# Feed-forward products of a two-layer encoder on one Trainium2 core: the 512-column products of a step first, then the 256-column ones, with start addresses of their own for the weight parts

## The chip, the cores and the metric

The kernel runs on 1 core of one Trainium2 chip. The metric is the device time of one execution in microseconds. Before the change the median of 3 runs is 1233.04 us (1232.77 to 1233.06).

## The reference

The reference is a trunk of two layers over 256 tokens of width 1024, in float32. Each layer computes two half-step feed-forwards with a group of mixers and a cross-attention between them:

```python
for l in range(DEPTH):
    x = x + 0.5 * swiglu(rms_norm(x, ffn1_norm_g[l]), ffn1_w1[l], ffn1_w3[l], ffn1_w2[l])
    ...
    x = x + jnp.concatenate([ret, hgo, lru], axis=-1) @ w_out[l]
    x = x + cross_attention(rms_norm(x, xattn_norm_g[l]), rms_norm(mem, xattn_mem_g[l]), ...)
    x = x + 0.5 * swiglu(rms_norm(x, ffn2_norm_g[l]), ffn2_w1[l], ffn2_w3[l], ffn2_w2[l])
return rms_norm(x, final_norm_g)

def swiglu(h, w1, w3, w2):
    return (jax.nn.silu(h @ w1) * (h @ w3)) @ w2
```

The feed-forward width D_FF is 2816, so w1 and w3 are 1024 x 2816 and w2 is 2816 x 1024. The change concerns the four feed-forwards.

## The kernel before

**Split numbers.** Every large product is made of matmuls in fp32r. A float32 operand is split into a hi part (the value rounded to fp32r) and a lo part (the rest), and a product x w is computed as hi·hi + hi·lo + lo·hi. For the weights, `Weights._split` (from L107) does this for one step of up to 1024 columns per partition: ScalarE casts the raw weights to `w_hi` (L126) and VectorE subtracts to get `w_lo` (L127). Raw weights come by DMA from SyncE's queue (L99) into two buffers of 1 MB; `w_hi` and `w_lo` have three buffers each (PART_BUFS).

**Activations.** The tile `xn` holds, for each of 8 blocks of 128 features, the hi part of 256 tokens and then the lo part, 512 columns in a row; `g` holds the same for the 22 blocks of the inner width. So for one block of weights that TensorE has loaded, one matmul with 512 moving columns gives hi·hi and hi·lo at once, in the two halves of a PSUM bank, and one matmul of 256 columns with the lo part of the weights is added into the second half. `mm_w` (from L259) issues this pair:

```python
def mm_w(self, wh, wl, x, begin, stop):
    self.mm(self.ap, wh, x, begin, stop)
    self.mm(self.ap[:, 1, :], wl, x[:, 0, :], False, stop)
```

**Loops.** `ffn` walks over 11 column pairs of w1 and w3 (256 columns of the inner width at a time). For each of the two matrices, `gemm_w` takes the steps of the weights (a step holds 4 blocks of the contraction by 256 columns) and for each of two output banks and each block of the step it calls `mm_w`. The two matrices have 8 blocks of contraction, so two steps; w2 has 22, five steps of four and one of two. The very first column pair of the program uses `gemm_both`, with smaller steps (1, 1, 2, 2 and 2 blocks of both matrices). A bank is evacuated by a copy of its second half on ScalarE (L493) and an addition of the first half on VectorE (L494), or, after w2, by two additions into `xT` (L466).

**Who sets the order.** The Tile framework schedules the instructions by a simulation of its own, by priority and readiness, so the order on an engine is near that of the code, but a product may stand ahead of another where an operand is late. All matmuls go through `Bank.mm`, so they have the line L243 in the profile (L241 where `issue_after` is used; L245 in the changed file).

**Addresses.** The tiles `xn`, `g`, `w_hi` and `w_lo` are allocated with some spare elements and used from an offset in them (`XN_AT`, `G_AT` and `W_AT`, in elements of 4 bytes; `W_AT` by the weights' name). In the built program the buffers of `w_hi` and `w_lo` begin at 128 modulo 256 bytes, `xn` at 64 and `g` at 160; steps inside a tile are multiples of 512 bytes, so all products of a kind have the same start modulo 256. The offset for the weights of the feed-forwards is 16 (128 + 64 = 192), for `xn` 8 (64 + 32 = 96), for `g` 48 (160 + 192 = 352, which is 96).

**Other stages that the prediction reads.** The second matrix of the last feed-forward is computed the other way round (`gemm_x`, from L389): the activations are loaded, and hi and lo parts of 512 weight columns stream, all at 64 modulo 256. The keys of the cross-attention (`gemm_n` with `mem_n`) use products of 256 columns only, the moving operand at 64 and the weights at 32. The attention's scores (`k_mem` and `att`) are 256-column products with both operands at 160.

Of the kernel before, what the change touches and what calls it, by code (L numbers as in the profile page):

```python
# [9 lines left out]
F32R = mybir.dt.float32r  # L10
# [5 lines left out]
P = 128  # L16
D = 1024
S = 256
KD = D // P
# [5 lines left out]
CW = 256  # L25
# [5 lines left out]
PART_BUFS = 3  # L31
# [2 lines left out]
QE_BUFS = 1  # L34
T3_BUFS = 8
PAD = {"xn": 16, "g": 128, "mix": 0}
XN_AT = {"ffn1": 8, "mix": 8, "xattn": 8, "ffn2": 8}

W_AT = {("w13", False): 16, ("w1", False): 16, ("w3", False): 16, ("w2", False): 16, ("w2", True): 48,
        ("in", True): 56, ("kv", False): 40, ("kv", True): 48, ("out", False): 0, ("o", False): 0, "other": 48}  # L40
G_AT = (48, 40)
MIX_AT = 0
X_LOADS = ((0, 1), (1, 1), (2, 2), (4, 2), (6, 2))
T4_BUFS = 6
# [17 lines left out]
class Weights:  # L62
# [45 lines left out]
    def _split(self):  # L108
        nc, i = self.nc, self.n_split
        self.n_split += 1  # L110
        u, unit, at, nk = self.steps[i]
        while self.n_load < len(self.pieces) and self.pieces[self.n_load][0] <= u:
            self._load()
        at_ = W_AT.get((unit.key, unit.beside), W_AT["other"])
        hi = self.pool.tile([P, 4 * CW + 64], F32R, name="w_hi", tag="w_hi", bufs=PART_BUFS)[:, at_:at_ + 4 * CW]
        lo = self.pool.tile([P, 4 * CW + 64], F32R, name="w_lo", tag="w_lo", bufs=PART_BUFS)[:, at_:at_ + 4 * CW]
        if unit.key == "w13":
            hi, lo = (t[:, 0:2 * nk * CW].rearrange("p (h k c) -> p h k c", h=2, k=nk) for t in (hi, lo))
            t = self._both(u, at).rearrange("p (h k c) -> p h k c", h=2, k=nk)
        elif unit.beside:  # L120
            hi, lo = (t.rearrange("p (h k c) -> p h k c", h=2, k=2)[:, :, 0:nk, :] for t in (hi, lo))
            t = self.raw[u].rearrange("p h (k c) -> p h k c", k=4)[:, :, at:at + nk, :]
        else:
            hi, lo = (t.rearrange("p (k c) -> p k c", k=4)[:, 0:nk, :] for t in (hi, lo))
            t = self.raw[u].rearrange("p h (k c) -> p h k c", k=4)[:, at, 0:nk, :]
        self.last = nc.scalar.copy(hi, t)  # L126
        nc.vector.tensor_tensor(out=lo, in0=t, in1=hi.bitcast(F32), op=ALU.subtract)  # L127
        self.parts[i] = (hi, lo)
# [88 lines left out]
def trunk(ctx: ExitStack, tc: tile.TileContext, a: dict, out: bass.AP, stop=None, dbg=None):  # L217
# [9 lines left out]
    class Bank:  # L227
# [28 lines left out]
            self.mm(acc, lh, rl, False, False)  # L256
            self.mm(acc, ll, rh, False, stop)

        def mm_w(self, wh, wl, x, begin, stop):  # L259

            self.mm(self.ap, wh, x, begin, stop)
            self.mm(self.ap[:, 1, :], wl, x[:, 0, :], False, stop)

    class Act:

# [23 lines left out]
    def placed(pool, name, k, at, **kw):  # L289

        n = k * 2 * S
        return pool.tile([P, n + PAD[name]], F32R, name=name, bufs=1, **kw)[:, at:at + n].rearrange(
            "p (k u s) -> p k u s", k=k, u=2)
# [34 lines left out]
    vec_off, n = {}, 0  # L328
# [36 lines left out]
    def gemm_w(key, nk, x, banks):  # L365

        k0 = 0
        while k0 < nk:
            wh, wl, n = W.take(key)
            for m, bank in enumerate(banks):  # L370
                for k in range(n):
                    sl = slice(m * P, (m + 1) * P)
                    bank.mm_w(wh[:, k, sl], wl[:, k, sl], x[:, k0 + k], k0 + k == 0, k0 + k == nk - 1)
            k0 += n
            yield

    def gemm_both(x, pairs):

        k0 = 0
        while k0 < KD:  # L380
            wh, wl, n = W.take("w13")
            for u, banks in enumerate(pairs):
                for m, bank in enumerate(banks):
                    for k in range(n):
                        sl = slice(m * P, (m + 1) * P)
                        bank.mm_w(wh[:, u, k, sl], wl[:, u, k, sl], x[:, k0 + k], k0 + k == 0, k0 + k == KD - 1)
            k0 += n

    def gemm_x(key, nk, x, banks):  # L389
# [36 lines left out]
    class Norm:  # L426


        def __init__(self, l, name, mem=False):
            self.gains = col(l, name)  # L430
            if not mem:
                self.x = placed(keep, "xn", KD, XN_AT[name.split("_")[0]], tag="xn")
            self.ssq = small.tile([P, S], F32, name="ssq", tag="ssq", bufs=2)
# [38 lines left out]
    def ffn(l, f, nrm, nxt, last=False, setup=None):  # L472
        with tc.tile_pool(name="ffn", bufs=2) as fp:
            g = placed(fp, "g", KF, G_AT[last])
            if setup is not None:
# [35 lines left out]
            for c in range(0, KD, 2):  # L511
                banks = [mm_bank(2) for _ in range(2)]
                run(gemm_w("w2", KF, g, banks))
                for m in range(2):
                    add_tile(c + m, [banks[m][:, u, :] for u in range(2)], 0.5, nxt)
# [660 lines left out]
    for l in range(DEPTH):  # L1176
# [6 lines left out]
        with tc.tile_pool(name="kvp", bufs=1) as kvp, tc.tile_pool(name="mix", bufs=T4_BUFS) as mp:  # L1183
            nxt = Norm(l, "xattn_norm_g")
            k = mixer(l, nrm, nxt, mp, kvp)
# [104 lines left out]
```

## Time and profile before

| | |
|---|---|
| median of 3 runs | 1233.04 us |
| the profiled execution, its own time | 1232.75 us |
| its span (first to last instruction) | 1231.0 us |
| granted TensorE clock, mean | 0.998 |
| TensorE busy | 1220.6 us, 8378 matmuls |
| VectorE busy | 935.7 us |
| ScalarE busy | 738.3 us |
| DMA | 219.32 MB, mean 178 GB/s |

The profile is of one execution. Matmuls are pipelined, so the busy time of one overlaps that of the next; how long a product holds the engine is read from the distance of two starts in the timeline.

### The profile page before, as it was taken

To read this page: it belongs to the slowest core of one execution; us is meant where nothing else is said; L and a number is where in the kernel's file an instruction comes from. 1 tells how busy PE (TensorE), PEld (TensorE's weight loads), DVE (VectorE), ACT (ScalarE), POOL (GpSimd) and SP (SyncE) were. 2 spreads that over 40 slices of the span, in tenths; PEclk is the share of its full clock that TensorE was granted. 3 is DMA by queue.
4 is the path that set the end of the run, shared out by engine and by line. 5 is a ranking of instruction groups with operands and counts; after the bars stand their busy time and mean duration, and the time that the engine had idled before them with its cause. 6 is when DMAs were issued, how large, how long until landed. Compare 5 with 4: busy or idle time off the path is not lost.

```text
span 1231.0 us, 21670 instructions
## 1 busy us (share of the span) xinstructions
PE 1220.6 (99%) x8378; PEld 1100.8 (89%) x8378; DVE 935.7 (76%) x1649; ACT 738.3 (60%) x1309; POOL 30.5 (2%) x54
## 2 busy tenths in 40 slices
PE   9999999999999999999999999999999999999997
PEld 8888889988999988888888888899898999888886
DVE  6989866888777687786678886679787767778754
ACT  6766645556765665664466654465677646656643
POOL 1000000000100000000000000000000000000000
PEclk9999999999999999999999999999999999999999
DMA  7645555443344345455555455544434534555453
GB/s 253 251 182 190 173 190 200 146 163 138 137 173 171 125 184 200 177 205 188 189 216 204 177 200 188 188 171 155 155 138 146 196 137 155 192 185 200 177 188 120
DMA packets 62568, 219.32 MB, mean 178 GB/s; under 512 B 6912, under 2 KB 8192, under 8 KB 62208
## 3 DMA queue, kind: packets, MB, share of 16 engines
q1 hardware_dynamic: 60976, 213.35, 47.6%
q0 software_dynamic: 768, 3.86, 0.8%
q8 instruction: 66, 1.08, 0.3%
q10 hardware_dynamic: 720, 0.72, 0.2%
q14 instruction: 38, 0.31, 0.1%
HBM read 216.85 MB, written 1.05 MB: 177 GB/s over the span
## 4 chain that ended last, share of the span: by engine, by line
PE 95%; DVE 3%; ACT 1%; issue 1%; DMA 0%; POOLq 0%; POOL 0%; ACTq 0%; DVEq 0%
PE mm L243 87%; PE aux L243 2%; PE aux L833 1%; DVE w_lo L127 1%; DVE qe L814 0%; PE aux L831 0%; DMA xT<-in_x_t_dram 0%; PE mm L241 0%; ACT w_hi L126 0%; PE aux L241 0%; DVE xc L908 0%; PE aux L826 0%; PE aux L983 0%; PE aux L912 0%; PE aux L1104 0%
## 5 line engine op out<-in xcount | busy, mean ns | idle before, releaser
L127 DVE TENSOR_TENSOR w_lo<-w_raw,w_hi 128x1024 fp32r<-128x1024 f32 (+1 forms) x411 | 494.6, 1205 | 213.5 <-ACT w_hi L126 208.3
L126 ACT CAST w_hi<-w_raw 128x1024 fp32r<-128x1024 f32 (+1 forms) x411 | 425.1, 1035 | 360.5 <-PE mm L243 217.6
L243 PE MATMUL mm<-xn,w_hi 128*128 128x512 f32 (+1 forms) x2028 | 601.1, 359 | 1.6 <-ACT ssq L440 0.9
L243 PE MATMUL mm<-xn,w_lo 128*128 128x256 f32 x1728 | 476.9, 281 | 0.0
L243 PEld LDWEIGHTS mm<-xn,w_hi 128*128 128x128 f32 x2028 | 357.6, 188 | 57.2 <-ACT w_hi L126 1.1
L243 PEld LDWEIGHTS mm<-xn,w_lo 128*128 128x128 f32 x1728 | 324.7, 188 | 3.7
L243 PE MATMUL mm<-g,w_hi 128*128 128x512 f32 x528 | 180.8, 392 | 0.0
L243 PE MATMUL mm<-g,w_lo 128*128 128x256 f32 x528 | 141.9, 280 | 0.0
L243 PEld LDWEIGHTS mm<-g,w_hi 128*128 128x128 f32 x528 | 96.6, 188 | 19.0
L243 PEld LDWEIGHTS mm<-g,w_lo 128*128 128x128 f32 x528 | 99.4, 188 | 2.9
L243 PE MATMUL mm<-w_hi,xn 128*128 128x512 f32 (+1 forms) x318 | 89.1, 374 | 0.0
L493 ACT COPY f_p<-mm 128x256 f32<-128x256 f32 x176 | 63.8, 365 | 24.5 <-PE mm L243 23.6
L494 DVE TENSOR_TENSOR f_t<-mm,f_p 128x256 f32<-128x256 f32 x176 | 73.1, 418 | 2.5 <-ACT f_p L493 2.4
L243 PEld LDWEIGHTS mm<-w_hi,xn 128*128 128x128 f32 x318 | 57.2, 188 | 9.2
L498 DVE TENSOR_TENSOR f_t<-f_t,R 128x512 f32<-128x512 f32 x88 | 60.2, 688 | 1.6 <-ACT R L462 0.4
L243 PE MATMUL mm<-w_lo,xn 128*128 128x512 f32 (+1 forms) x160 | 56.6, 378 | 1.0 <-DVE w_lo L127 1.0
L243 PE MATMUL mm<-w_hi,g 128*128 128x512 f32 x176 | 51.9, 390 | 0.0
L243 PE MATMUL mm<-mem_n,w_hi 128*128 128x256 f32 x248 | 46.7, 284 | 0.0
L243 PE MATMUL mm<-o,w_hi 128*128 128x256 f32 x248 | 46.2, 281 | 0.0
L466 DVE SCALAR_TENSOR_TENSOR xT<-mm,xT 128x256 f32<-128x256 f32 x80 | 32.1, 420 | 17.3 <-PE mm L243 17.3
L243 PE MATMUL mm<-mix,w_hi 128*128 128x256 f32 x256 | 44.8, 279 | 0.0
L243 PE MATMUL mm<-w_hi,mem_n 128*128 128x512 f32 x128 | 39.5, 393 | 0.0
(253 smaller groups left out, 1476.6 us busy)
## 6 DMA issues: line engine op xcount, KB each, us to landing
w_raw<-in_weights_dram SPq DMA_DIRECT2D x395, 512.0 KB, 4.0
w_raw<-in_weights_dram SPq DMA_DIRECT2D x18, 256.0 KB, 3.6
m_t<-in_mem_t_dram POOLq DMA_DIRECT2D x2, 1024.0 KB, 6.4
xT<-in_x_t_dram SPq DMA_DIRECT2D x3, 256.0 KB, 6.4
cst<-in_c_cst_dram POOLq DMA_DIRECT2D x1, 696.0 KB, 4.4
out_dram<-yg SPq DMA_DIRECT2D x2, 320.0 KB, 2.5
gw<-in_gates_w_dram POOLq DMA_DIRECT2D x2, 256.0 KB, 6.8
fg<-in_final_norm_g_dram POOLq DMA_DIRECT2D x1, 512.0 KB, 5.8
```

The source lines that it names most:

```text
L126: self.last = nc.scalar.copy(hi, t)
L127: nc.vector.tensor_tensor(out=lo, in0=t, in1=hi.bitcast(F32), op=ALU.subtract)
L243: i = self.last = nc.tensor.matmul(acc, lhsT, rhs, start=begin, stop=stop, skip_group_check=True)
L466: nc.vector.scalar_tensor_tensor(out=xT[:, j, :], in0=h, scalar=scale, in1=xT[:, j, :], op0=ALU.mult, op1=ALU.add)
L493: nc.scalar.copy(p, banks[m][:, 1, :])
L494: nc.vector.tensor_tensor(out=t[m][:, u, :], in0=banks[m][:, 0, :], in1=p, op=ALU.add)
L498: nc.vector.tensor_tensor(out=t[m], in0=t[m], in1=nrm.R[:, None, :].to_broadcast([P, 2, S]), op=ALU.mult)
L833: nc.tensor.matmul(sb[bs, i, :], ke[:, 1 + i, cb], qe[:, 1 + i, cb], start=True, stop=True, skip_group_check=True)
```

## The change

`mm_w` now takes a list of the blocks of a step and issues all products with the hi part first, then all products with the lo part. `gemm_w` and `gemm_both` pass the list. `W_AT` has an offset each for the hi and the lo part; for the feed-forwards these are 48 and 40 instead of 16 and 16. The offset of `xn` is 0 instead of 8 in the feed-forwards, that of `g` is 40 instead of 48 in the first three.

```diff
-XN_AT = {"ffn1": 8, "mix": 8, "xattn": 8, "ffn2": 8}
-
-W_AT = {("w13", False): 16, ("w1", False): 16, ("w3", False): 16, ("w2", False): 16, ("w2", True): 48,
-        ("in", True): 56, ("kv", False): 40, ("kv", True): 48, ("out", False): 0, ("o", False): 0, "other": 48}
-G_AT = (48, 40)
+XN_AT = {"ffn1": 0, "mix": 8, "xattn": 8, "ffn2": 0}
+
+W_FF = (48, 40)
+W_AT = {("w13", False): W_FF, ("w1", False): W_FF, ("w3", False): W_FF, ("w2", False): W_FF, ("w2", True): (48, 48),
+        ("in", True): (56, 56), ("kv", False): (40, 40), ("kv", True): (48, 48), ("out", False): (0, 0),
+        ("o", False): (0, 0), "other": (48, 48)}
+G_AT = (40, 40)
...
-        hi = self.pool.tile([P, 4 * CW + 64], F32R, name="w_hi", tag="w_hi", bufs=PART_BUFS)[:, at_:at_ + 4 * CW]
-        lo = self.pool.tile([P, 4 * CW + 64], F32R, name="w_lo", tag="w_lo", bufs=PART_BUFS)[:, at_:at_ + 4 * CW]
+        hi = self.pool.tile([P, 4 * CW + 64], F32R, name="w_hi", tag="w_hi", bufs=PART_BUFS)[:, at_[0]:at_[0] + 4 * CW]
+        lo = self.pool.tile([P, 4 * CW + 64], F32R, name="w_lo", tag="w_lo", bufs=PART_BUFS)[:, at_[1]:at_[1] + 4 * CW]
...
-        def mm_w(self, wh, wl, x, begin, stop):
-
-            self.mm(self.ap, wh, x, begin, stop)
-            self.mm(self.ap[:, 1, :], wl, x[:, 0, :], False, stop)
+        def mm_w(self, steps):
+
+
+            for wh, _, x, begin, stop in steps:
+                self.mm(self.ap, wh, x, begin, stop)
+            for _, wl, x, _, stop in steps:
+                self.mm(self.ap[:, 1, :], wl, x[:, 0, :], False, stop)
...
-                for k in range(n):
-                    sl = slice(m * P, (m + 1) * P)
-                    bank.mm_w(wh[:, k, sl], wl[:, k, sl], x[:, k0 + k], k0 + k == 0, k0 + k == nk - 1)
+                sl = slice(m * P, (m + 1) * P)
+                bank.mm_w([(wh[:, k, sl], wl[:, k, sl], x[:, k0 + k], k0 + k == 0, k0 + k == nk - 1)
+                           for k in range(n)])
```

`gemm_both` is changed in the same way. In the built programs the start addresses of the changed products, modulo 256 bytes, are:

| product | moving, loaded before | moving, loaded now |
|---|---|---|
| xn with w_hi, 512 columns | 96, 192 | 64, 64 |
| xn with w_lo, 256 columns | 96, 192 | 64, 32 |
| g with w_hi, 512 columns | 96, 192 | 64, 64 |
| g with w_lo, 256 columns | 96, 192 | 64, 32 |

No other product gets another address.

TensorE, in the middle of a feed-forward (layer 0, the second one; `mm_5204` is a bank, `w_hi_5143` and `w_lo_5144` the parts of one step), before:

```order
L243 MATMUL mm_5204<-xn_4326,w_hi_5143 128x512
L243 MATMUL mm_5204<-xn_4326,w_lo_5144 128x256
L243 MATMUL mm_5204<-xn_4326,w_hi_5143 128x512
L243 MATMUL mm_5204<-xn_4326,w_lo_5144 128x256
L243 MATMUL mm_5204<-xn_4326,w_hi_5143 128x512
L243 MATMUL mm_5204<-xn_4326,w_lo_5144 128x256
L243 MATMUL mm_5204<-xn_4326,w_hi_5143 128x512
L243 MATMUL mm_5204<-xn_4326,w_lo_5144 128x256
```

and now:

```order
L245 MATMUL mm_5204<-xn_4326,w_hi_5143 128x512 x4
L245 MATMUL mm_5204<-xn_4326,w_lo_5144 128x256 x4
L245 MATMUL mm_5204<-xn_4326,w_hi_5163 128x512 x4
L245 MATMUL mm_5204<-xn_4326,w_lo_5164 128x256 x4
L245 MATMUL mm_5205<-xn_4326,w_hi_5143 128x512 x4
L245 MATMUL mm_5205<-xn_4326,w_lo_5144 128x256 x4
```

The alternation of the two sizes has become groups of four of each. In the built program there are 394 runs of four 512-column products and 439 runs of four 256-column products; most others are runs of two, at the ends of w2, or longer ones.

TensorE in the first unit of the program (`gemm_both`; four banks, `w_hi_144` holds two blocks of both matrices), before:

```order
L243 MATMUL mm_164<-xn_126,w_hi_144 128x512
L243 MATMUL mm_165<-xn_126,w_hi_144 128x512
L243 MATMUL mm_166<-xn_126,w_hi_144 128x512
L243 MATMUL mm_167<-xn_126,w_hi_144 128x512
L243 MATMUL mm_164<-xn_126,w_lo_145 128x256
L243 MATMUL mm_164<-xn_126,w_hi_144 128x512
L243 MATMUL mm_164<-xn_126,w_lo_145 128x256
L243 MATMUL mm_165<-xn_126,w_lo_145 128x256
```

and now:

```order
L245 MATMUL mm_164<-xn_126,w_hi_144 128x512 x2
L245 MATMUL mm_165<-xn_126,w_hi_144 128x512 x2
L245 MATMUL mm_166<-xn_126,w_hi_144 128x512 x2
L245 MATMUL mm_167<-xn_126,w_hi_144 128x512 x2
L245 MATMUL mm_164<-xn_126,w_lo_145 128x256 x2
L245 MATMUL mm_165<-xn_126,w_lo_145 128x256 x2
L245 MATMUL mm_166<-xn_126,w_lo_145 128x256 x2
L245 MATMUL mm_167<-xn_126,w_lo_145 128x256 x2
```

Four 512-column products stood in a row here before, too; the last product of every bank of a step now stands behind all products with the hi part.

TensorE at the start of the second feed-forward of layer 0, where the last block of `xn` is first used (the fourth product with `w_hi_5024` of bank `mm_5087`), before:

```order
L243 MATMUL mm_5139<-xn_4326,w_hi_5112 128x512
L243 MATMUL mm_5087<-xn_4326,w_hi_5024 128x512
L243 MATMUL mm_5087<-xn_4326,w_lo_5025 128x256
L243 MATMUL mm_5088<-xn_4326,w_hi_5024 128x512
L243 MATMUL mm_5088<-xn_4326,w_lo_5025 128x256
L243 MATMUL mm_5087<-xn_4326,w_hi_5024 128x512
L243 MATMUL mm_5087<-xn_4326,w_lo_5025 128x256
L243 MATMUL mm_5088<-xn_4326,w_hi_5024 128x512
```

and now:

```order
L245 MATMUL mm_5139<-xn_4326,w_hi_5112 128x512
L245 MATMUL mm_5087<-xn_4326,w_hi_5024 128x512
L245 MATMUL mm_5088<-xn_4326,w_hi_5024 128x512
L245 MATMUL mm_5138<-xn_4326,w_hi_5112 128x512
L245 MATMUL mm_5139<-xn_4326,w_hi_5112 128x512
L245 MATMUL mm_5087<-xn_4326,w_hi_5024 128x512
L245 MATMUL mm_5087<-xn_4326,w_lo_5025 128x256 x4
```

The scheduler takes the 512-column products of four banks in turn, block by block, and the 256-column products of a bank come behind the last block. The orders of SyncE and GpSimd are the same as before; on VectorE and ScalarE a few evacuations and casts have changed places with their neighbours.

## Rows read from the trace of the kernel before

**Rows 1.** The page: span, and busy time of engines (share) xinstructions.

```profile
span 1231.0 us, 21670 instructions
PE 1220.6 (99%) x8378; PEld 1100.8 (89%) x8378; DVE 935.7 (76%) x1649; ACT 738.3 (60%) x1309; POOL 30.5 (2%) x54
```

**Rows 2.** The page: the chain that ended last, by engine and by line.

```profile
PE 95%; DVE 3%; ACT 1%; issue 1%; DMA 0%; POOLq 0%; POOL 0%; ACTq 0%; DVEq 0%
PE mm L243 87%; PE aux L243 2%; PE aux L833 1%; DVE w_lo L127 1%; DVE qe L814 0%; PE aux L831 0%; DMA xT<-in_x_t_dram 0%; PE mm L241 0%; ACT w_hi L126 0%; PE aux L241 0%; DVE xc L908 0%; PE aux L826 0%; PE aux L983 0%; PE aux L912 0%; PE aux L1104 0%
```

**Rows 3.** Windows of two feed-forwards: busy us by engine, clock, DMA share.

```profile
core 0: us, PE busy (x) PEld busy (x) DVE busy (x) ACT busy (x) POOL busy (x), PEclk, DMA share, GB/s
...
455.00:610.00 155.00, 155.00 (x896) 136.44 (x895) 116.46 (x182) 87.16 (x148) 0.00 (x0) 1.00 0.52 189
640.00:795.00 155.00, 155.00 (x895) 136.46 (x895) 120.40 (x194) 90.68 (x155) 0.00 (x0) 1.00 0.52 190
```

**Rows 4.** Groups of TensorE by form: xcount, busy us, mean ns, idle before.

```profile
L243 PE MATMUL mm<-xn,w_hi 128*128 128x512 f32 x1408 | 486.9, 393 | 1.6 <-ACT ssq L440 0.9 <-DVE xn L361 0.7
L243 PE MATMUL mm<-xn,w_lo 128*128 128x256 f32 x1728 | 476.9, 281 | 0.0
L243 PE MATMUL mm<-g,w_hi 128*128 128x512 f32 x528 | 180.8, 392 | 0.0
```

**Rows 5.** Timeline of TensorE in a feed-forward: start us, us, what.

```profile
499.92 0.39 PE L243 MATMUL mm<-xn,w_hi 128*128 128x512 f32 x1
500.15 0.28 PE L243 MATMUL mm<-xn,w_lo 128*128 128x256 f32 x1
500.27 0.39 PE L243 MATMUL mm<-xn,w_hi 128*128 128x512 f32 x1
...
503.04 0.39 PE L243 MATMUL mm<-xn,w_hi 128*128 128x512 f32 x1
```

**Rows 6.** Timeline of TensorE, last feed-forward's second matrix, 24 products between these.

```profile
1189.99 0.62 PE L243 MATMUL mm<-w_hi,g 128*128 128x512 f32 x2
...
1195.43 0.62 PE L243 MATMUL mm<-w_hi,g 128*128 128x512 f32 x2
```

**Rows 7.** Timeline of TensorE, the keys, 26 products between these.

```profile
302.32 0.39 PE L243 MATMUL mm<-mem_n,w_hi 128*128 128x256 f32 x2
...
305.35 0.28 PE L243 MATMUL mm<-mem_n,w_lo 128*128 128x256 f32 x1
```

**Rows 8.** Timeline of TensorE in the first unit: four in a row.

```profile
10.47 1.09 PE L243 MATMUL mm<-xn,w_hi 128*128 128x512 f32 x4
11.40 0.28 PE L243 MATMUL mm<-xn,w_lo 128*128 128x256 f32 x1
```

**Rows 9.** Timeline of TensorE, the attention's scores: six products (5 and 1).

```profile
391.25 0.76 PE L243 MATMUL aux<-k_mem,att 128*128 128x256 f32 x5
...
391.97 0.76 PE L243 MATMUL aux<-k_mem,att 128*128 128x256 f32 x5
```

**Rows 10.** Timeline of VectorE while the keys' weights are split.

```profile
305.23 1.23 DVE L127 TENSOR_TENSOR w_lo<-w_raw,w_hi 128x1024 fp32r<-128x1024 f32 x1 [1.09 <-ACT w_hi L126]
```

**Rows 11.** Timeline at the start of layer 0's second feed-forward.

```profile
432.73 0.64 PE L243 MATMUL mm<-xn,w_hi 128*128 128x512 f32 x2
...
436.16 1.28 DVE L361 SCALAR_TENSOR_TENSOR xn<-xT,vec,xn 128x256 fp32r<-128x256 f32 x3
...
440.87 0.39 PE L243 MATMUL mm<-xn,w_hi 128*128 128x512 f32 x1
```

**Rows 12.** Timeline of TensorE at the end of the first unit.

```profile
18.74 0.28 PE L243 MATMUL mm<-xn,w_lo 128*128 128x256 f32 x1
18.94 0.50 PE L243 MATMUL mm<-xn,w_hi 128*128 128x512 f32 x1
19.28 0.28 PE L243 MATMUL mm<-xn,w_lo 128*128 128x256 f32 x1
```

More of the change, by code (lines that the diff above doesn't have):

```diff
@@ L383, in gemm_both @@
                 for m, bank in enumerate(banks):
-                    for k in range(n):
-                        sl = slice(m * P, (m + 1) * P)
-                        bank.mm_w(wh[:, u, k, sl], wl[:, u, k, sl], x[:, k0 + k], k0 + k == 0, k0 + k == KD - 1)
+                    sl = slice(m * P, (m + 1) * P)
+                    bank.mm_w([(wh[:, u, k, sl], wl[:, u, k, sl], x[:, k0 + k], k0 + k == 0, k0 + k == KD - 1)
+                               for k in range(n)])
             k0 += n
```

## Prediction

> **What bounds the kernel now.** I read the page's first part, then the chain, then the windows of the feed-forwards. TensorE is busy for 1220.6 of the 1231.0 us; VectorE has 76% of the span [rows 1]. The chain that ended last lies on TensorE for 95%, and 87% of it is one helper line, L243, which issues the products [rows 2]. In two feed-forward stretches TensorE has no idle time at all (155.00 of 155.00 us) at a granted clock of 1.00, its 2.4 GHz level, while VectorE is at 116 to 120 us, ScalarE at 87 to 91 and DMA at about half [rows 3]. So in these stages nothing is waited for: the time is the number of products times the slot that each takes, from its start to the next one's start. (The "mean ns of one" is no slot: consecutive matmuls overlap in it.)
>
> I call a product of 512 columns H and one of 256 columns L. The change touches 1408 + 528 = 1936 H [rows 4] and as many L (the L row of xn, x1728, also holds 320 of the mixer and attention). In today's alternating order nine pairs start between 499.92 and 503.04, so a pair takes 3.12 / 9 = 0.3467 us; the H slot is 0.23 and the L slot 0.12 [rows 5]. The 1936 pairs are 671 us, more than half of the kernel. One nanosecond per pair is 1.9 us.
>
> **The change, part by part.**
>
> *Order.* It removes and adds no instruction, byte or semaphore; inside a step the four H of a bank now stand together and the four L behind them. Today's trace has stages that already run products of one size in a row, and they show what such slots cost. The second matrix of the last feed-forward runs H alone: 24 of them from 1189.99 to 1195.43, 226.7 ns each [rows 6]. The keys of the cross-attention run L alone: 26 from 302.32 to 305.35, 116.5 ns each [rows 7]. Together 343.2 against 346.7.
>
> *Addresses.* Those two stages differ from the changed products in where their operands begin. In the first, moving and stationary operand both begin at 64 modulo 256 bytes [rows 6]; in the second at 64 and 32 [rows 7]. Today's feed-forward products begin at 96 and 192, and in the one place where they stand four in a row, in the first unit, four H take 11.40 - 10.47 = 0.93 us, 232.5 each [rows 8]: more than the 230 of the alternation. So the order by itself, at the old addresses, is not a gain. The change gives H the pair 64 and 64, that of rows 6, and L the pair 64 and 32, that of rows 7. I therefore price an H followed by an H at 226.7 and an L followed by an L at 116.5. What speaks against it: in rows 6 the weights stream and the activations are loaded, in the changed products it is the other way round.
>
> *The two turns of each group.* An H followed by an L, and an L followed by an H, have no row at the new addresses. Bounds for the H: 226.7 [rows 6] and 232.5 [rows 8]; I take 230, the H of the alternation, which is followed by an L too [rows 5]. For the L, which now streams while a stationary operand is loaded from the same start modulo 256: the attention's scores are 256-column products with equal starts and take 0.72 / 6 = 120 ns [rows 9]; the other bound is 116.5. I take 117, today's L before an H [rows 5].
>
> *The sum.* A group of four pairs takes 4 x 346.7 = 1386.7 ns now, and then 3 x 226.7 + 230 + 3 x 116.5 + 117 = 1376.6: 10.1 less. There are 344 such groups in the first two matrices (8 in each of 44 column pairs, without the 8 of the first unit) and 5 in each of the 24 output tiles of the second matrix, 464 in all: 4.7 us. Groups of two (24 in the second matrix, 12 in the first unit) save 693.3 - 690.2 = 3.1 each, 0.1 us. With the dear turns (230 and 120) a group saves 7.1, and the whole is 3.3; with the cheap ones (226.7 and 116.5) 13.9, and the whole 6.7. Sum: 4.8 us, from 3.3 to 6.7.
>
> *Edits that I cost at nothing.* The cast and the subtraction write the same number of elements, 1024, to another start; a subtraction into w_lo takes 1.23 us where the offset is already 40 [rows 10]. If that were wrong, VectorE has 35 us of idle time in 155 [rows 3] as cover. The lo part is needed 3 x 0.23 = 0.7 us later in each step than today, which only adds slack; today's waits for it are already none in these stretches [rows 3].
>
> *Where cover is lost.* At the start of a feed-forward the tiles of xn arrive one by one, and an L of an early tile can no longer fill a wait for a later one, since it stands behind the four H. At the second feed-forward of layer 0 the last tile is written by 436.16 + 1.28 = 437.44, and the first H that needs it starts at 440.87 [rows 11]. In the new order 28 H and 16 L stand ahead of that H, 28 x 0.2267 + 16 x 0.1165 = 8.2 us from 432.73, so 440.9 again: 3.5 us of slack are kept, and I cost it at 0. In the first unit a bank's last product moves to the end, so its evacuation starts later; there TensorE waits some 0.2 us today (an L slot of 0.20 and an H slot of 0.34 instead of 0.12 and 0.23 [rows 12]). The two small products of the norm now stand in that place and fill part of it. Bounds: -0.2 us, the wait goes, and +0.2, it doubles; I take 0.
>
> *Against the clock.* The profiled execution took 1232.75 us (span 1231.0), 0.29 less than the median of 1233.04. 1232.75 - 4.8 = 1227.95, and 1228.2 on the scale of the median. 1228.2 is my forecast.
>
> **A rule that speaks against it.** Slots at one and the same clock differ with the start addresses: 226.7 against 232.5 for four or more H in a row [rows 6, 8]. The Trainium skill, "TensorE: Matmul & The Clock Gate", sections "Back-to-back issue gap" and "What happens when you issue a matmul", gives the gap as columns / 2.4 + 2.5 ns and says that loading the next weights takes no read bandwidth from the running product. By it a pair is 325 ns in every order and at every address, the change is worth 0, and the time stays 1233.0. The trace does not agree: no pair is at 325, and slots of one size are not equal.
>
> **The rivals.**
>
> *No change.* The slot goes with which operand streams, not with the addresses: 226.7 is a property of streaming weights. Then an H in a run of the changed products stays near 230 and an L near 117, a pair near 347, and the time is between 1232.5 and 1233.5. For it: every stage with 226.7 streams weights. Against it: if only that mattered, the H of rows 8 would be at 230 as well, and not at 232.5. The rule of the Trainium skill above ends at the same time.
>
> *Slower.* Standing in a row is what costs: the runs of the first unit repeat at the new addresses, because that is how activations stream past freshly loaded weights. A group is then 4 x 232.5 + 4 x 117 = 1398, 11.3 more than now, times 464 is 5.2 us: 1238.3. It decides from the point at which an H inside a run is over 229.7 (4 x 229.7 + 4 x 117 = 1386.8). For it: rows 8 is the only place in this trace with the same operands in the same order. Against it: the start pair there is 96 and 192, and every stage with equal starts runs H at about 227.
>
> *The order is not what it says.* The scheduler could take the runs apart; the built order shows runs of four H in 394 places and of four L in 439, with the rest mostly longer, so I give it nothing.
>
> **How the numbers follow.** A measurement of this kernel tells some 0.2% (2.5 us) from no change, so faster means under 1230.6 and slower over 1235.5. The forecast has 0.66, no change 0.25 (0.05 of it for a case between the two, in which only a part of the address gain comes and the time ends between 1230.6 and 1232.5), slower 0.09. The forecast's own range is 1226.1 (the cheap turns, and 0.2 us of wait gone) to 1229.9 (the dear turns, and 0.2 us of new wait). Up to 1233.2 the range takes in the no-change case, and 0.3 us below the cheap end allow for the reading of the rows, whose starts are given to 0.01 us; it leaves out the slower rival and little else: 1225.8 to 1233.2. Faster 0.66, same 0.25, slower 0.09.
>
> **What would show it.** In the second feed-forward of layer 0 the profile should show H in rows of four taking 0.91 us from first to last start plus one, and a group of eight repeating every 1.377 us instead of 1.387. TensorE should stay busy for the whole of such a stretch, and idle time should not move to L126 or L127. If H starts lie 0.230 apart, the no-change rival holds; at 0.2325, the slower one. If the slots come out as forecast but the span does not shrink by 4 to 5 us, a wait at a stage's start has taken it, and the first products on xn would show it.

## The result and the profile after

The changed kernel takes 1242.54 us (median of 5 runs, 1242.37 to 1243.21) where the kernel before took 1232.77 beside it (5 runs, 1232.39 to 1233.06). The ratio is 1.0080, interval 1.0069 to 1.0092: slower by 9.8 us. The forecast was 1228.2 with a range to 1233.2, so it is wrong in sign, and the time lies beyond the slower rival's 1238.3 too.

The page of the changed kernel, span and busy time of the engines, which answers to [rows 1]:

```profile
span 1240.8 us, 21657 instructions
PE 1230.1 (99%) x8378; PEld 1100.6 (89%) x8378; DVE 937.1 (76%) x1649; ACT 741.7 (60%) x1309; POOL 32.3 (3%) x54
```

The span grew by 9.8 and TensorE's busy time by 9.5, with the same 8378 matmuls. TensorE's idle time went from 10.4 to 10.7 us. So nothing new is waited for: the products themselves take longer.

The same windows as [rows 3], busy time by engine, clock and DMA share:

```profile
core 0: us, PE busy (x) PEld busy (x) DVE busy (x) ACT busy (x) POOL busy (x), PEclk, DMA share, GB/s
...
455.00:610.00 155.00, 155.00 (x881) 134.37 (x880) 115.55 (x181) 88.08 (x149) 0.00 (x0) 1.00 0.51 185
640.00:795.00 155.00, 155.00 (x880) 134.25 (x879) 120.31 (x195) 91.56 (x157) 0.00 (x0) 1.00 0.52 188
```

TensorE is busy throughout, at the same granted clock of 1.00, but it gets through 881 and 880 products in 155 us where it did 896 and 895: 1.7% fewer. The reader should compare the counts in brackets here; the busy column alone says nothing has changed.

The waits of TensorE, the longest ones (us in total, times, longest):

```profile
PE mm L245 <- DVE xn L358: 1.3, 1, 1.3
PE aux L329 <- DVE mhalf L331: 1.0, 1, 1.0
PE mm L245 <- DVE w_lo L129: 1.0, 2, 0.5
PE mm L245 <- DVE xn L366: 0.7, 1, 0.7
```

The wait for a subtraction was there before, by the same view:

```profile
PE mm L243 <- DVE w_lo L127: 1.0, 2, 0.5
```

No wait is over 1.3 us, and no idle time has moved to the casts or the subtractions (L128 and L129 now).

The timeline of TensorE in the second feed-forward of layer 0 (start, us from first start to last end, products in the row), where [rows 5] showed the alternation:

```profile
502.17 1.10 PE L245 MATMUL mm<-xn,w_hi 128*128 128x512 f32 x4
503.11 0.64 PE L245 MATMUL mm<-xn,w_lo 128*128 128x256 f32 x4
503.58 1.10 PE L245 MATMUL mm<-xn,w_hi 128*128 128x512 f32 x4
504.53 0.63 PE L245 MATMUL mm<-xn,w_lo 128*128 128x256 f32 x4
505.00 0.40 PE L245 MATMUL mm<-xn,w_hi 128*128 128x512 f32 x1
```

The order is what the change says: four H, four L. From 502.17 to 505.00 two groups pass, 1.415 us each; the forecast was 1.377 and the kernel before has 1.387. A row of four H takes 0.94 to 0.95 us, and not 0.91. With the trace's starts, averaged over some 300 rows of four H on xn, the four slots are 240.4, 237.2, 233.0 and 230.9 ns, and of the L 118.3, 119.0, 115.9 and 117.3. That makes 941.5 + 470.5 = 1412 ns a group, 25.3 more than before. The built order has 394 rows of four H: 394 x 25.3 = 10.0 us, the size of the whole loss. Adding up the slots of all products of both traces says the same without a mean: the 1408 H on xn take 7.5 us longer, the 528 H on g 2.2 us, and the L together no longer than before. The loss lies in the H.

### The profile page after: what moved, and what is told of

Read it like the earlier page. It is cut to its first block, busy times and chain, and to the rows that moved or that the text cites. A ratio compares the mean times of both kernels' runs of the same rounds, so it can differ in the third digit from the quotient of the medians.

```text
span 1240.8 us, 21657 instructions
## 1 busy us (share of the span) xinstructions
PE 1230.1 (99%) x8378; PEld 1100.6 (89%) x8378; DVE 937.1 (76%) x1649; ACT 741.7 (60%) x1309; POOL 32.3 (3%) x54
## 4 chain that ended last, share of the span: by engine, by line
PE 95%; DVE 2%; ACT 1%; issue 1%; DMA 0%; POOLq 0%; POOL 0%; SPq 0%; DVEq 0%; ACTq 0%
PE mm L245 88%; PE aux L245 2%; PE aux L838 1%; DVE w_lo L129 0%; DMA w_raw<-in_weights_dram 0%; PE aux L836 0%; ACT w_hi L128 0%; PE mm L243 0%; PE aux L243 0%; PE aux L831 0%; PE aux L988 0%; PE aux L917 0%; PE aux L1109 0%; PE aux L974 0%; DVE qe L819 0%
## 5 line engine op out<-in xcount | busy, mean ns | idle before, releaser
L129 DVE TENSOR_TENSOR w_lo<-w_raw,w_hi 128x1024 fp32r<-128x1024 f32 (+1 forms) x411 | 494.2, 1204 | 213.4 <-ACT w_hi L128 209.2
L128 ACT CAST w_hi<-w_raw 128x1024 fp32r<-128x1024 f32 (+1 forms) x411 | 424.9, 1034 | 344.0 <-PE mm L245 232.1
L245 PE MATMUL mm<-xn,w_hi 128*128 128x512 f32 (+1 forms) x2028 | 502.5, 362 | 1.9 <-DVE xn L358 1.3
L245 PEld LDWEIGHTS mm<-xn,w_hi 128*128 128x128 f32 x2028 | 336.9, 188 | 38.3 <-ACT w_hi L128 1.4
L245 PE MATMUL mm<-xn,w_lo 128*128 128x256 f32 x1728 | 313.7, 281 | 0.0
L245 PEld LDWEIGHTS mm<-xn,w_lo 128*128 128x128 f32 x1728 | 275.5, 188 | 30.2
L245 PE MATMUL mm<-g,w_hi 128*128 128x512 f32 x528 | 145.5, 396 | 0.0
L245 PEld LDWEIGHTS mm<-g,w_hi 128*128 128x128 f32 x528 | 89.7, 188 | 12.2
L245 PEld LDWEIGHTS mm<-g,w_lo 128*128 128x128 f32 x528 | 81.2, 188 | 12.1
L245 PE MATMUL mm<-g,w_lo 128*128 128x256 f32 x528 | 84.0, 280 | 0.0
```

Source lines behind the costliest of these rows:

```text
L245: i = self.last = nc.tensor.matmul(acc, lhsT, rhs, start=begin, stop=stop, skip_group_check=True)
```

## The experiments

The kernel before measured 1232.5 to 1232.8 us beside every run below. Slots are from the trace's starts, averaged over all rows of a kind on xn. "Settled" means the slot that a long row keeps from its sixth product on, the last product aside. Every edit is shown against the changed kernel; `...` marks lines left out.

### The two halves of the change alone

The order alone, at the old addresses:

```diff
-XN_AT = {"ffn1": 0, "mix": 8, "xattn": 8, "ffn2": 0}
+XN_AT = {"ffn1": 8, "mix": 8, "xattn": 8, "ffn2": 8}
...
-W_FF = (48, 40)
+W_FF = (16, 16)
...
-G_AT = (40, 40)
+G_AT = (48, 40)
```

> The new order (four H, then four L) at the addresses of before (96 and 192). Theory 'turns': an H costs 226.7 ns only once a run has settled, and every run of H pays behind a run of L, whatever the addresses; then this is slow as well, about 1238 to 1243 us, with H slots over 230 in every group. Theory 'addresses': the new start pairs are the loss; then this stays at 1233 us or below, and the four H of a group take no more than 920 ns.

Measured: 1242.70 us (1242.37 to 1243.24), ratio 1.0083 (1.0066 to 1.0100). H 231.2, 234.6, 233.4, 235.2; L 118.4, 118.4, 120.3, 118.3: 1410 a group.

The addresses alone, in the old order:

```diff
-            for wh, _, x, begin, stop in steps:
+            for wh, wl, x, begin, stop in steps:
                 self.mm(self.ap, wh, x, begin, stop)
-            for _, wl, x, _, stop in steps:
                 self.mm(self.ap[:, 1, :], wl, x[:, 0, :], False, stop)
```

> The old order (H, L, H, L) at the new addresses (64 and 64 for H, 64 and 32 for L). Theory 'turns': the alternation keeps its own rhythm, a pair stays within 1 ns of 346.7 and the time within 1231 to 1235 us. Theory 'addresses': the pair rises by some 5 ns as in the changed kernel, and the time is 1240 us or more.

Measured: 1242.53 us (1242.40 to 1242.58), ratio 1.0080 (1.0065 to 1.0095). H 232.9, L 120.1: 353.0 a pair. The timeline of the addresses alone, nine pairs between the rows:

```profile
500.14 0.40 PE L245 MATMUL mm<-xn,w_hi 128*128 128x512 f32 x1
...
503.33 0.39 PE L245 MATMUL mm<-xn,w_hi 128*128 128x512 f32 x1
```

3.19 / 9 = 354 ns, against 346.7 in [rows 5]. So each half costs some 10 us alone, and both together cost 10 and not 20. The halves do not add: neither "the turns of a row cost" nor "the addresses cost" explains the result without the other. Here the L lose as well: added up over the trace, the slots of all H grew by 6.0 us and those of the L by 4.0, which is the whole loss.

### Longer rows

Rows of eight: the H of both banks, then the L of both, at the new addresses.

```diff
+        def mm_hi(self, steps):
+            for wh, _, x, begin, stop in steps:
+                self.mm(self.ap, wh, x, begin, stop)
+
+        def mm_lo(self, steps):
+            for _, wl, x, _, stop in steps:
+                self.mm(self.ap[:, 1, :], wl, x[:, 0, :], False, stop)
...
             for m, bank in enumerate(banks):
-                sl = slice(m * P, (m + 1) * P)
...
+                bank.mm_hi(steps[m])
+            for m, bank in enumerate(banks):
+                bank.mm_lo(steps[m])
```

> At the new addresses all eight H of a step (both banks) come before all eight L. Theory 'turns': half as many turns; eight H take about 1832 ns and eight L about 931, as in the nine places of the changed kernel where this already occurs, 10 ns less than eight pairs in alternation, so about 1230 us, faster than before. Theory 'addresses': all H slots stay high (235 on the mean) and the time stays near 1242 us.

Measured: 1235.79 us (1235.13 to 1238.09), ratio 1.0026 (1.0017 to 1.0036). The loss falls from 9.8 to 3.1. The slots by place in the row, H: 232.8, 235.7, 228.3, 232.6, 230.5, 226.9, 226.7, 235.0. The sixth and the seventh are at the forecast's 226.7; the first five and the last are not.

The expected 1230 was missed by 6 us. It took eight H at 1832 ns from the nine places of the changed kernel where they stand in a row; here they take 1848.5. Those nine places stand among rows of other lengths (from the changed kernel's trace, at the end of an output tile of the second matrix):

```profile
577.99 0.63 PE L245 MATMUL mm<-g,w_lo 128*128 128x256 f32 x4
578.46 1.99 PE L245 MATMUL mm<-g,w_hi 128*128 128x512 f32 x8
580.29 1.10 PE L245 MATMUL mm<-g,w_lo 128*128 128x256 f32 x8
581.22 1.09 PE L245 MATMUL mm<-g,w_hi 128*128 128x512 f32 x4
582.14 0.64 PE L245 MATMUL mm<-g,w_lo 128*128 128x256 f32 x4
582.62 1.10 PE L245 MATMUL mm<-g,w_hi 128*128 128x512 f32 x4
583.56 0.63 PE L245 MATMUL mm<-g,w_lo 128*128 128x256 f32 x4
```

Eight H behind four L take 1.83 us here; four H take 0.92 us behind eight L and 0.94 behind four. Against 226.7 for each H, the nine rows of eight are 18 ns dearer and the nine rows of four behind them 19. In the kernel with rows of eight, rows of eight H that stand behind only four L are 55 ns dearer (15 rows), and those behind eight L 35. So what a row of H costs over the settled slot depends on the rows ahead of it.

Does streaming activations reach 226.7 at all? In this kernel every L is replaced by a second H with the same operands (the lo part of the weights is left out, and the hi part counted twice); the first feed-forwards have the new addresses, the second ones the old.

```diff
-            for _, wl, x, _, stop in steps:
-                self.mm(self.ap[:, 1, :], wl, x[:, 0, :], False, stop)
+            for wh, _, x, _, stop in steps:
+                self.mm(self.ap, wh, x, False, stop)
...
```

> The feed-forwards (but for the last second matrix) compute something else here: each product with the lo part of the weights is replaced by a second H with the same operands, so TensorE runs H alone; the first feed-forward of a layer is at the new addresses, the second one at those of before. The time is longer by the replaced columns and says nothing. Theory 'turns': an H at the new addresses takes 226.7 ns over hundreds of products, with activations streaming; at the old ones a run of H stays at about 232.5. Theory 'addresses': an H stays at 231 or more at the new ones too, since it is the streaming operand that decides.

Measured: 1451.79 us in one run, for 1936 products of 512 columns where there were 256. The timeline of TensorE, first a first feed-forward (40 H from xn, up to the first of g), then a stretch of a second one:

```profile
159.66 9.23 PE L247 MATMUL mm<-xn,w_hi 128*128 128x512 f32 x40
168.73 31.44 PE L247 MATMUL mm<-g,w_hi 128*128 128x512 f32 x138
```

```profile
574.63 65.76 PE L247 MATMUL mm<-xn,w_hi 128*128 128x512 f32 x280
```

At the new addresses 9.07 / 40 = 226.8 ns each, at the old (65.76 - 0.39) / 279 = 234.3. So in a long row 226.7 comes with the starts and not with the operand that streams, as the forecast had it; and long rows of H at 96 and 192 are dearer than the 230 of the alternation, which is why the order alone lost: its four H sum to 934.4, 233.6 each. That is not over the settled 234.3, so at the old starts the H of a row of four carry no price for the turn.

### The old order at other starts

A first theory after these runs was that a slot goes with the operand that is loaded beside it, which is the next product's. Three kernels in the old order, with the loop of "the addresses alone", and one in the new order, with other starts of hi and lo; of the edits only the starts are shown:

```diff
-W_FF = (48, 40)
+W_FF = (40, 48)
```

> The old order (H and L alternately), with the two starts of the weights exchanged: the hi part begins at 32 and the lo part at 64 modulo 256, activations at 64. Theory A, the load beside: a slot goes with the start of the streaming operand against the start of the stationary operand that is loaded beside it, which is the next product's. Beside an H the lo part (64) is loaded, equal starts: H 226.7; beside an L the hi part (32): L 116.5 to 117. A pair is 343.2 to 343.7, 3.0 to 3.5 less than the kernel before, over 1936 pairs 5.8 to 6.8 us: 1226 to 1227. Theory B, the product's own load: a slot goes with the start of its own stationary operand: H at 64 with 32 gives 233, L at 64 with 64 gives 120, a pair 353 as with the unexchanged starts: 1242.5. Theory C, the rhythm: changing sizes in turn costs, whatever the starts, so a pair stays at 346.7 or more: 1233 or later.

Measured: 1229.63 us (9 runs, 1229.52 to 1229.97), ratio 0.9974 (0.9965 to 0.9984): 3.1 us faster than the kernel before, the best time of the study. H 227.3, L 118.0: 345.2 a pair (hi at 32, lo at 64). Its timeline, nine pairs:

```profile
499.86 0.39 PE L245 MATMUL mm<-xn,w_hi 128*128 128x512 f32 x1
500.08 0.28 PE L245 MATMUL mm<-xn,w_lo 128*128 128x256 f32 x1
500.20 0.39 PE L245 MATMUL mm<-xn,w_hi 128*128 128x512 f32 x1
...
502.95 0.39 PE L245 MATMUL mm<-xn,w_hi 128*128 128x512 f32 x1
```

3.09 / 9 = 343 ns here, 345.2 as the mean over all. Windows of the first feed-forward and of the one with these rows show part of the difference (busy time by engine, clock, DMA share):

```profile
30.00:185.00 155.00, 155.00 (x897) 136.59 (x896) 129.41 (x262) 97.19 (x173) 0.72 (x1) 1.00 0.54 196
455.00:610.00 155.00, 155.00 (x901) 137.26 (x900) 116.69 (x183) 87.45 (x148) 0.00 (x0) 1.00 0.53 190
```

In the first 100 us the same products with the same starts run H at 227 to 234 (means over 20 us), 231 in all, and from then on at 226 to 228: 897 products in the first window, 901 in the second. The sign is theory A's, but the L is dearer than it says, and the next three runs refute it. Theory C, which had 346.7 or more, falls here.

```diff
-W_FF = (48, 40)
+W_FF = (48, 48)
```

> The old order, hi and lo both beginning at 64 modulo 256, activations at 64. Theory A, the load beside: every product streams from 64 beside a load from 64: H 226.7, L 120, a pair 346.7, the same as the kernel before: 1233. Theory B, the product's own load: the same starts, so the same numbers. Theory C, the rhythm: an H after an L stays at 230 or more, a pair 350 or more: over 1239.

Measured: 1241.69 us (1240.88 to 1242.51), ratio 1.0072 (1.0053 to 1.0090). H 235.1, L 116.8. Every product has equal starts, its own and its neighbour's, and H is nowhere near 226.7. Theories A and B fall.

```diff
-W_FF = (48, 40)
+W_FF = (40, 40)
```

> The old order, hi and lo both beginning at 32 modulo 256, activations at 64. Theory A, the load beside, and theory B, the own load, agree here: H 233, L 116.5 to 117, a pair 349.5 to 350: 1238 to 1239. Theory C, the rhythm: no number of its own, 346.7 or more. With this run and the one with both at 64, the price of each of the four combinations stands alone; if the exchanged run is the sum of the cheap two, A holds.

Measured: 1233.66 us (1233.42 to 1233.90), ratio 1.0007 (0.9997 to 1.0017). H 228.8, L 118.2: 347.0 where A and B had 350.

The new order with `W_FF = (40, 48)`, hi at 32 and lo at 64:

> The order of the changed kernel (four H, then four L), with the two starts exchanged: hi at 32, lo at 64. Theory A, the load beside: three H of a group run beside a load from 32 and one beside a load from 64, three L beside 64 and one beside 32: 3 x 233 + 226.7 + 3 x 120 + 117 = 1403 per group, 16 more than the kernel before, 7.5 us: 1240. Theory B, the own load: 4 x 233 + 4 x 120 = 1412: 1244. Theory C, the rhythm: the first H after a run of L are slow whatever the starts, so 1410 as in the three arrangements seen so far: 1242 to 1243.

Measured: 1236.25 us (1235.93 to 1237.18), ratio 1.0029 (1.0018 to 1.0040). H 228.5, 234.9, 231.1, 235.5; L 116.2, 112.8, 116.9, 118.2: 1394 a group. No theory had that; A, at 1240, was the nearest and still 4 us off.

### All starts at once

In these two kernels the starts change from unit to unit of the first two matrices, through all 64 combinations; the first in the old order, the second in the new.

```diff
         at_ = W_AT.get((unit.key, unit.beside), W_AT["other"])
+        if unit.key in ("w1", "w3"):
+            n_ff = sum(k in ("w1", "w3") for k in self.keys[:u])
+            at_ = (n_ff % 8 * 8, (n_ff + n_ff // 8) % 8 * 8)
```

> The old order, activations at 64; in the first two matrices the starts of hi and lo change from unit to unit (16 pairs each) through all 64 combinations of 0, 32, ... 224 modulo 256; the second matrix as in the changed kernel. The slots by combination are read, not the time. Seen so far per pair (hi, lo): 64, 32: 353.0; 64, 64: 351.8; 32, 64: 345.2; 32, 32: 347.0. Theory D, the start of the part that H loads: the pair goes with hi, and lo moves it by less than 2 ns: eight columns of nearly equal numbers, from 345 to 353. Theory E, the distance between the two stationary starts: the pair goes with hi minus lo, so combinations of equal distance agree; the two equal starts seen so far, 351.8 and 347.0, speak against it. Theory F, history: the slot depends on the starts of all neighbours and on when each begins, so the table has no simple law and neighbouring combinations differ by up to 10 ns.

> The same scan in the order of the changed kernel, four H and then four L. Seen so far per group of four pairs (hi, lo): 64, 32: 1412; 32, 64: 1396; both at 192 with activations at 96: 1410. If a row of four could be priced from long rows by its own starts, as the prediction did, then hi 64 would give 4 x 226.7 = 907 for the H of a group at least in some lo, and the L 466 to 470. Theory D: the group goes with hi alone. Theory F, history: the first H after four L is over 226.7 in every combination, the sum of four H is over 915 in all 64, and no group is below the 1387 of the kernel before.

Measured, in one run each (1238.80 and 1239.34 us), from the units that stand undisturbed in the trace (in rows of four these cover 59 of the 64 combinations): in the old order a pair takes 340.1 to 353.8 ns, with no order in rows or columns of the table; theories D and E find nothing in it. In rows of four a group takes 1384.2 to 1430.5 ns as the mean of a unit. Averaged over a unit, the cheapest four H sum to 919.8 where the forecast had 910. Theory F misses in two places: the first H is under 226.7 at (hi, lo) = (0, 32) and (128, 192), 225.8 in both; and the one unit at (0, 0) has a group at 1384.2, with two of its four rows at 912. All others are over the 1386.7 of the kernel before. So the scan shows no choice of the two starts, with activations at 64, that makes rows of four more than 2.5 ns a group cheaper; that none would gain over a whole kernel is not shown, as the next run warns.

The cheapest combination of the first scan was then given to all products:

```diff
-W_FF = (48, 40)
+W_FF = (0, 48)
```

> The old order, hi beginning at 128 and lo at 64 modulo 256, activations at 64, in all three matrices: the cheapest combination of the alternating scan, 340.1 ns a pair over 16 pairs of one unit (H 227.0, L 113.1). If the slot is a fixed property of the starts in an order, that holds over all 1936 pairs: 6.6 less than the 346.7 of the kernel before, 12.8 us: 1220. If it depended on what the neighbouring units of the scan left behind, a pair comes back toward the mean of the scan, some 349: 1233 or later, and nothing is gained.

Measured: 1236.62 us (1235.91 to 1236.93), ratio 1.0031 (1.0019 to 1.0044). H 231.5, L 117.4: 348.9 where one unit of the scan had shown 340.1. A slot of the alternation is not a fixed property of its starts. The scan put other units ahead of this one, so what ran before seems to count too; in any case 16 pairs of a scan do not price a kernel.

### What a turn costs

Rows of sixteen, at the addresses of the change: two steps of weights are taken together (and split one step less ahead).

```diff
-SPLIT_AHEAD = PART_BUFS
+SPLIT_AHEAD = 2
...
+            steps = [[] for _ in banks]
+            for _ in range(min(2, -(-(nk - k0) // 4))):
+                wh, wl, n = W.take(key)
+                for m in range(len(banks)):
...
+                k0 += n
             for m, bank in enumerate(banks):
...
+                bank.mm_hi(steps[m])
+            for m, bank in enumerate(banks):
+                bank.mm_lo(steps[m])
```

> The addresses of the changed kernel, with rows of sixteen H and sixteen L (two steps of weights taken together; rows of twelve at the end of the second matrix). If the length of the row decides, the first five and the last H of a row are as in rows of eight and all between are at 226.7: 16 H take 1848.5 + 8 x 226.7 = 3662, 16 L take 931.5 + 8 x 116.5 = 1863.5, a pair 345.3 against 347.5 in rows of eight and 353.0 in rows of four: 1230 to 1231, if the weights, now split one step less ahead, cause no new wait. If instead the activations' streaming never settles beside fresh loads, a pair stays at 347.5 or more: 1234 or later.

Measured: 1230.38 us (10 runs, 1230.07 to 1231.18), ratio 0.9981 (0.9972 to 0.9990). The same addresses that lost 9.8 us in rows of four gain 2.4 in rows of sixteen. The timeline of TensorE:

```profile
500.18 3.82 PE L245 MATMUL mm<-xn,w_hi 128*128 128x512 f32 x16
503.84 2.03 PE L245 MATMUL mm<-xn,w_lo 128*128 128x256 f32 x16
505.70 3.82 PE L245 MATMUL mm<-xn,w_hi 128*128 128x512 f32 x16
509.37 2.03 PE L245 MATMUL mm<-xn,w_lo 128*128 128x256 f32 x16
511.23 3.82 PE L245 MATMUL mm<-xn,w_hi 128*128 128x512 f32 x16
```

From 500.18 to 511.23 are 32 pairs: 345.3 each, as worked out beforehand. By the starts, 16 H take 3661.4 (expected 3662) and 16 L 1865.1 (expected 1863.5). H by place: 232.6, 235.7, 228.4, 232.6, 230.8, then ten between 226.6 and 226.7, and 235.0 for the last. By the code, the weights in such a row come from another tile after every four H and the output goes to another bank after eight; the slots from the sixth on show neither.

Two more, also in rows of sixteen, separate what changes at a turn. With both parts at 64, only the size of the product changes there; with both at 32, activations and weights never start alike:

```diff
-W_FF = (48, 40)
+W_FF = (48, 48)
```

> Rows of sixteen with hi and lo both beginning at 64 modulo 256. Theory S, the change of start: nothing changes at a turn but the size, so every H is at 226.7 from the first, 16 H 3627, and the L at equal starts settle at 120: 16 L 1920, a pair 346.7: 1232.8. Theory T, the change of size: the first five H and the last remain dear, 16 H about 3661, with L at 120 a pair 348.8: 1236 to 1237.

Measured: 1234.85 us (1234.56 to 1235.27), ratio 1.0018 (1.0008 to 1.0028). H: 233.2, 235.9, 228.3, 232.5, 230.9, then 226.4 to 227.0 up to and with the last, 226.5; L 113.5, 119.0, then 120. Neither theory holds whole. The five dear H at the head of a row come with the change of size, since no start changes here (theory T). The dear last H does come from the start: it is 235.0 before a lo part at 32, and 226.5 before one at 64 (theory S).

```diff
-W_FF = (48, 40)
+W_FF = (40, 40)
```

> Rows of sixteen with hi and lo both beginning at 32 modulo 256, activations at 64. If a long row of H needs equal starts to settle at 226.7, the H stay at 230 to 235 through the row (the last H of a row, beside a load from 32, takes 235): 16 H 3680 to 3760, 16 L 1865, a pair 346.6 to 351.6: 1232.5 to 1242. If the length of the row alone decides, the H settle at 226.7 here too: a pair 345.3, 1230.4 as in the rows of sixteen at 64 and 32.

Measured: 1238.22 us (1238.12 to 1238.29), ratio 1.0044 (1.0026 to 1.0062). The H alternate between 234.5 and 232.2 to the end of the row, 3732.8 for sixteen, and none at its head is dearer than the rest: the dear head of theory T is seen at 64 only. The timelines of the last two, a row of sixteen H and the start of the L behind it, both at 64 and then both at 32:

```profile
501.01 3.82 PE L245 MATMUL mm<-xn,w_hi 128*128 128x512 f32 x16
504.66 2.08 PE L245 MATMUL mm<-xn,w_lo 128*128 128x256 f32 x16
```

```profile
502.00 3.89 PE L245 MATMUL mm<-xn,w_hi 128*128 128x512 f32 x16
505.73 2.03 PE L245 MATMUL mm<-xn,w_lo 128*128 128x256 f32 x16
```

3.65 against 3.73 us for the same sixteen H. So of the long rows tried, only those with equal starts, 64 and 64, settle at 226.7. The L is the other way round: 16 take 1912 at equal starts and 1867 at 64 and 32.

## Why the prediction was wrong

**The step that failed is the price of an H followed by an H, 226.7 ns, under "Addresses".** It is the slot of settled rows, and the forecast gave it to three of the four H of every row. They took 240.4, 237.2 and 233.0: 30.5 ns of the 35.4 by which a group came out dearer than forecast (1412 against 1376.6). The L followed by an L, 116.5 from settled rows too, took 118.3, 119.0 and 115.9: 3.7 more. The two terms under "The two turns of each group" were nearly right by themselves: 230 for the H before an L measured 230.9, 117 for the L before an H measured 117.3; for the H that is luck, since the last H of longer rows takes 235.0. So the forecast charged a turn to the product in front of it, 3.3 + 0.5 = 3.8 ns over the settled slots for both turns, and the runs show it mostly in the slots behind it: none of the four H of a row settles, and in long rows the first five are dear, and the last. With the settled 226.7 and 116.5 taken off, all at the addresses of the change, in rows of equal length:

| row | H of a row | over 226.7 each | L of a row | over 116.5 each | per pair |
|---|---|---|---|---|---|
| forecast, four | 910.1 | 3.3 | 466.5 | 0.5 | 344.2 |
| four (changed kernel) | 941.5 | 34.7 | 470.5 | 4.5 | 353.0 |
| eight | 1848.5 | 34.9 | 931.5 | -0.5 | 347.5 |
| sixteen | 3661.4 | 34.2 | 1865.1 | 1.1 | 345.4 |

Where H and L rows of one length follow one another, the excess of the H is 34 to 35 ns a row, for four, eight and sixteen alike. It is the turn's price there, and it was put ten times too low. It is no constant: among rows of unlike length it was 18 to 55 ns for a row of eight (above), and at the old starts there is none. Settled slots save 346.7 - 343.2 = 3.5 ns a pair, so such a row has to be some ten pairs long before it pays, an estimate that lies between the eight that lost and the sixteen that gained; four pairs save 14 ns and cost 39. That is 25.3 a group, the number of the trace.

**What had shown it.** The forecast read 226.7 from a stage with 24 H in a row [rows 6], and put the only four H in a row with the same operands [rows 8], 232.5 each, down to their starts. Both readings were of two things at once, length and starts. The runs separate them: at the old starts a settled H is 234.3, so [rows 8] was right about its starts; at the new starts a row of four averages 235.4, so [rows 6] said nothing about a row of four.

**The slower rival** was right in kind (a row's H over the 229.7 from which it decides) and half the size: it carried over 232.5 and 117, 1398 a group, and found 5.2 us. It also gave itself a wrong reason against, that stages with equal starts run H at about 227; the old order with both parts at 64 has equal starts everywhere and runs H at 235.1. The chance of 0.09 was too low for the one row of the trace that had the same operands in the same order.

**Point by point.** *Addresses*: the pair 226.7 and 116.5 is right for settled rows (the H doubled, rows of sixteen), and for no H in a row of four. *Order*: "the order by itself, at the old addresses, is not a gain" is right, and worse than was said, 1410 a group where 232.5 and 117 make 1398. *The sum*: its count of groups, 464, included those that the scheduler put together; with 394 rows of four the trace's 25.3 makes 10.0 of the measured 9.8. *Edits at nothing* and *Where cover is lost*: TensorE's idle time changed by 0.3 us and VectorE's busy time in the window 640 to 795 by 0.1, so these terms held. *The rule that speaks against it*: by the gap that the Trainium skill, "TensorE: Matmul & The Clock Gate", gives in "Back-to-back issue gap", columns / 2.4 + 2.5 ns, a pair is estimated at 325 ns in any order. No run here agrees: a pair ranged from 345.2 to 353.0 over whole kernels, with the same products.

## What to carry to other kernels

A slot read from a long row of equal products prices only a long row: ask how many products stand between two changes of size, and price the change itself. Here, at the new starts, it was 35 ns a row among rows of equal length, and another number among others. An order that groups products by size still lost 3.1 us with eight pairs and gained 2.4 with sixteen; four pairs were no better than the alternation at the same starts (1242.5 us both). Where an engine has no idle time in a window, compare the number of instructions in it, not its busy time.

## What the runs showed of the hardware

Averaged by place in a row, the same 512 columns took between 224 ns (fifth in a row of eight behind four L) and 241 (first behind four L) at a granted clock of 1.00, with no wait in the profile before them, depending on the start addresses modulo 256 bytes of the moving and the loaded operand and on what stood ahead. In the old order a pair took, over whole kernels with activations at 64 and (hi, lo) at the starts given:

| (32, 64) | (32, 32) | (128, 64) | (64, 64) | (64, 32) |
|---|---|---|---|---|
| 345.2 | 347.0 | 348.9 | 351.8 | 353.0 |

Inside rows the slots repeat by place, so the pattern is no noise: the heads of rows of eight and of sixteen H are alike, 232.8, 235.7, 228.3, 232.6, 230.5 and 232.6, 235.7, 228.4, 232.6, 230.8, although behind four L a row begins with 240.4 and 237.2. In the old order the same starts can run in more than one pattern (means of 226 to 234 for the H in one execution, above). What in the chip makes it is open. The traces show when a load and a product start, not how their reads meet; and the starts of the activations were tried at two values only, 64 and 96.
